# Row sums of a 64 MiB tensor: moving six of eight blocks from two engines to VectorE alone

## The chip, the cores and the metric

The kernel runs on one core of one Trainium2 chip. The metric is the device time of one execution in microseconds (us); a profile shows a span about 1.8 us shorter. Before the change the median was 162.4 us (162.32 to 162.68). All runs, each on one core, were at a granted clock of 1.0. They come from three chips; where a ratio is given, both kernels ran on the same chip in the same rounds.

Engine names in the profiles: DVE is VectorE, ACT is ScalarE, SPq is the sequencer of SyncE, which issues the DMAs. L92 is line 92 of that kernel; lines move by two or more between kernels. A *landing* is the moment when a whole block has arrived; it is read here as the start of DVE's reduction of that block, since DVE waits for each one.

## The reference

```python
x = np.random.randn(32, 512, 1024).astype(np.float32)      # 16384 rows, 67.1 MB
out = (np.sum(x, axis=-1) * 0.5).astype(np.float32)        # one number per row, 64 KB
```

Every input byte is read once and used for one addition, so the first question is how well the loads are kept running.

## The kernel before

The rows are laid over 128 partitions, 128 rows on each, in 8 blocks of 16 rows a partition (8.39 MB a block). A pool of three buffers holds the blocks. A load is one DMA of a whole block (64 KB for each partition); the last block comes in five pieces so that little is left to do after the last byte. In each block DVE reduces half the rows in one instruction, and ACT the other half, one row per instruction (a copy with scale whose accumulator gives the sum).

```python
B = 16                                       # rows of a partition in one block
x_pool = ctx.enter_context(tc.tile_pool(name="x", bufs=3))
# ... (cut: sums, res, part; act_row: one nc.scalar.activation(..., accum_out=res[:, col]) per row)
for b in range(n_blocks - 1):                # blocks 0 to 6
    c0 = b * B
    t = x_pool.tile([P, B, D], fp32, name="xb")
    loads.append(nc.sync.dma_start(out=t, in_=x_rows[:, c0 : c0 + B, :]))
    h = B // 2
    nc.vector.reduce_sum(out=sums[:, c0 : c0 + h], in_=t[:, 0:h, :], axis=mybir.AxisListType.X)
    nc.vector.tensor_single_scalar(out=res[:, c0 : c0 + h], in_=sums[:, c0 : c0 + h],
                                   scalar=mul, op=mybir.AluOpType.mult)
    for r in range(h, B):
        act_row(t, r, c0 + r)
# ... (cut: block 7 in five loads; 7 rows on ACT, the others on DVE; two stores)
```

A buffer may be loaded again when both engines have finished with it. With three buffers, the load of block b+3 is issued when block b is summed, while the loads of blocks b+1 and b+2 are already in the DMA queue.

Of the kernel before, what the change touches and what calls it, by code (L numbers as in the profile page):

```python
# [1 line left out]

# [4 lines left out]


@with_exitstack
def kernel(  # L10
    ctx: ExitStack,
    tc: tile.TileContext,
    x: bass.AP,
    multiplier: float,
    out: bass.AP,
):








    nc = tc.nc
    P = nc.NUM_PARTITIONS
    fp32 = mybir.dt.float32
    ADD = mybir.AluOpType.add

    x_flat = x.flatten_outer_dims()  # L30
    N, D = x_flat.shape
    rows = N // P
    out_flat = out.rearrange("b s -> (b s)")
    mul = float(multiplier)

    B = 16
    n_blocks = rows // B
    assert N == P * rows and rows == n_blocks * B
    own = rows - B
    x_rows = x_flat[0 : P * own, :].rearrange("(p c) d -> p c d", p=P)  # L40
    x_last = x_flat[P * own : N, :].rearrange("(p c) d -> p c d", p=P)
    out_rows = out_flat[0 : P * own].rearrange("(p c) -> p c", p=P)
    out_last = out_flat[P * own : N].rearrange("(p c) -> p c", p=P)

    x_pool = ctx.enter_context(tc.tile_pool(name="x", bufs=3))
    res_pool = ctx.enter_context(tc.tile_pool(name="res", bufs=1))
    sums = res_pool.tile([P, rows], fp32, name="sums")
    res = res_pool.tile([P, rows], fp32, name="res")
    part = res_pool.tile([P, 1], fp32, name="part")

    SYNC = mybir.DependencyInfo(mybir.DependencyClass.Sync, mybir.DependencyReason.DATA)
    ORDER = mybir.DependencyInfo(
        mybir.DependencyClass.NoSync, mybir.DependencyReason.SCHED_ONLY
    )

    def nop_after(engine, waits_for, follows):
        i = engine.nop()
        for w in waits_for:
            tc.add_manual_dep(i.ins, w.ins.name, SYNC, reason="end seen here")
        for f in follows:  # L60
            tc.add_manual_dep(i.ins, f.ins.name, ORDER, reason="in this order")
        return i

    loads = []
    acts = []

    def act_row(t, r, col):
        acts.append(nc.scalar.activation(  # L68
            out=t[:, r, :],
            in_=t[:, r, :],  # L70
            func=mybir.ActivationFunctionType.Copy,
            scale=mul,
            accum_out=res[:, col : col + 1],
        ))

    def dve_span(t, r, lo, hi, dst, start=0.0):
        mid = (lo + hi) // 2
        return nc.vector.tensor_tensor_reduce(  # L78
            out=t[:, r, lo:mid],
            in0=t[:, r, lo:mid],  # L80
            in1=t[:, r, mid:hi],
            scale=mul,
            scalar=start,
            op0=ADD,
            op1=ADD,
            accum_out=dst,
        )

    for b in range(n_blocks - 1):
        c0 = b * B  # L90
        t = x_pool.tile([P, B, D], fp32, name="xb")
        loads.append(nc.sync.dma_start(out=t, in_=x_rows[:, c0 : c0 + B, :]))  # L92
        h = B // 2
        nc.vector.reduce_sum(  # L94
            out=sums[:, c0 : c0 + h], in_=t[:, 0:h, :], axis=mybir.AxisListType.X
        )
        nc.vector.tensor_single_scalar(  # L97
            out=res[:, c0 : c0 + h],
            in_=sums[:, c0 : c0 + h],
            scalar=mul,  # L100
            op=mybir.AluOpType.mult,
        )
        for r in range(h, B):
            act_row(t, r, c0 + r)

    c0 = (n_blocks - 1) * B
    t = x_pool.tile([P, B, D], fp32, name="xb")
    cut = 576
    pieces = [(0, 8), (8, 13), (13, 15)]
    for lo, hi in pieces:  # L110
        loads.append(
            nc.sync.dma_start(  # L112
                out=t[:, lo:hi, :], in_=x_last[:, lo:hi, :]
            )
        )
    for lo, hi in ((0, cut), (cut, D)):
        loads.append(
            nc.sync.dma_start(  # L118
                out=t[:, B - 1, lo:hi], in_=x_last[:, B - 1, lo:hi]
            )  # L120
        )
    early = nc.sync.dma_start(out=out_rows, in_=res[:, 0:own])
    on_act = {4, 5, 6, 7, 11, 12, 14}
    for r in range(B - 1):
        if r in on_act:
            act_row(t, r, c0 + r)
        else:
            dve_span(t, r, 0, D, res[:, c0 + r : c0 + r + 1])
    dve_span(t, B - 1, 0, cut, part)
    final = dve_span(t, B - 1, cut, D, res[:, rows - 1 : rows], start=part)  # L130




    seen = nop_after(nc.sync, loads[-8:] + acts[-1:], [])
    store = nc.sync.dma_start(out=out_last, in_=res[:, own:])
    tc.add_manual_dep(store.ins, seen.ins.name, ORDER, reason="in this order")
    for a in acts[-len(on_act) :]:
        tc.declare_no_dep(store.ins, a.ins.name, reason="waited for by the nop in front")
    nop_after(nc.sync, [early, final], [store])  # L140

    def start_loads_at_entry(nc_):



        entry, *rest = nc_.main_func.blocks
        is_sp = lambda i: i.engine == mybir.EngineType.SP
        is_load = lambda i: type(i).__name__ == "InstDMACopy"
        for block in rest:
            body = list(block.instructions)  # L150
            own = [i for i in body if is_sp(i)]
            if not any(is_load(i) for i in own):
                continue
            lead = []
            for i in own:
                if not is_load(i) or i.sync_info.on_wait:
                    break
                lead.append(i)
            names = {i.name for i in lead}
            block.instructions = [i for i in body if i.name not in names]  # L160
            head = list(entry.instructions)
            at = next(
                k for k, i in enumerate(head) if is_sp(i) and type(i).__name__ == "InstDrain"
            )
            entry.instructions = head[:at] + lead + head[at:]
            return

    nc.at_finalize(start_loads_at_entry)


# [1 line left out]
_INS = ['x', 'multiplier']  # L172
_OUTS = [((32, 512), 'float32')]

_NUMBERS = {'multiplier': 0.5}


# [26 lines left out]
```

## Time and profile before

| | before |
|---|---|
| time, median | 162.4 us |
| DVE busy, ACT busy | 68.1 us, 67.9 us of a 160.6 us span |
| one block: from landing to landing | 19.35 us (one of the six intervals: 19.71) |
| one block: DVE's reduction | 8.69 us |
| reload issued after the landing of its buffer's block | 8.8 us |

The first lines are from the page of the kernel before: busy times; DMA queues; the chain of work that ended last, by engine; and the two costliest groups of instructions, where the number after the bar is busy time and the mean of one in ns, and behind the next bar the idle time in front of them and what ended it.

```profile
DVE 68.1 (42%) x34; ACT 67.9 (42%) x127; POOL 0.2 (0%) x4
...
q1 hardware_dynamic: 2016, 67.18, 97.4%
q14 instruction: 1, 0.01, 0.0%
...
DMA 86%; DVE 11%; SPq 1%; issue 0%; DVEq 0%
...
L68 ACT ACTIVATE xb<-xb 128x1024 f32<-128x1024 f32 x63 | 65.6, 1043 | 88.1 <-DMA xb<-in_x_dram 88.1
L94 DVE TENSOR_REDUCE sums<-xb 128x8 f32<-128x8192 f32 x7 | 60.8, 8686 | 84.9 <-DMA xb<-in_x_dram 84.9
```

Neither engine is busy half of the time, and what each waits for, 85 to 88 us in all, is the next load. The data queue takes 97.4% of the DMA engines' time. So the loads set the time. Note also the second queue: one packet of 0.01 MB on a queue called "instruction".

Next, windows of the kernel before, cut at four landings. A line has the window and its length, then the busy time of DVE, ACT and POOL, the granted clock, the share of the DMA engines and their rate in GB/s.

```profile
41.14:60.49 19.35, 8.86 (x2) 8.43 (x16) 0.00 (x0) 1.00 1.00 434
60.49:79.86 19.37, 8.86 (x3) 8.42 (x16) 0.00 (x0) 1.00 1.00 433
79.86:99.57 19.71, 8.86 (x3) 8.42 (x16) 0.00 (x0) 1.00 0.98 426
99.57:118.92 19.35, 8.86 (x3) 8.43 (x16) 0.00 (x0) 1.00 1.00 434
```

The DMA engines are full (1.00) at 434 GB/s. The Trainium skill, "DMA: Bandwidth & Descriptors", Specifications, gives 435 GB/s as the ceiling of the path into SBUF; this trace agrees with it. One interval is 0.36 us longer than the others.

The timeline of the kernel before around block 1 shows how a buffer comes free (columns: start, length, engine, line, operation; the idle time before in brackets).

```profile
41.14 8.69 DVE L94 TENSOR_REDUCE sums<-xb 128x8 f32<-128x8192 f32 x1 [10.43 <-DMA xb<-in_x_dram]
49.86 0.17 DVE L97 TENSOR_SCALAR res<-sums 128x8 f32<-128x8 f32 x1
49.91 0.33 SPq L92 DMA_DIRECT2D xb<-in_x_dram  x1
60.49 8.69 DVE L94 TENSOR_REDUCE sums<-xb 128x8 f32<-128x8192 f32 x1 [10.46 <-DMA xb<-in_x_dram]
```

Block 1 lands at 41.14, its sum ends 8.7 us later, and the reload of its buffer is issued at 49.91. At that moment 60.49 - 49.91 = 10.6 us of block 2's load are left, and all of block 3's, 19.35 us: 30 us of queued transfers. DVE then idles 10.4 us.

### The profile page before, as it was taken

How to read it: one execution, taken by the hardware profiler on the slowest of the kernel's cores; microseconds unless marked ns; L12 is line 12 of the kernel's file. 1: busy time of each engine (PE TensorE's matmuls, PEld its weight loads, DVE VectorE, ACT ScalarE, POOL GpSimd, SP SyncE). 2: the span in 40 equal slices, each digit the busy share in tenths (PEclk: the TensorE clock that was granted, in tenths of full speed). 3: DMA queues.
4: the chain of work that ended last, by engine and by line, in shares of the span. 5: the costliest groups of instructions: out<-in, count | busy, mean ns of one | idle time of the engine just before them, and what ended most of it. 6: DMA issues, size and time to landing. Idle time of an engine off the chain costs nothing.

```text
span 160.6 us, 236 instructions
## 1 busy us (share of the span) xinstructions
DVE 68.1 (42%) x34; ACT 67.9 (42%) x127; POOL 0.2 (0%) x4
## 2 busy tenths in 40 slices
DVE  0000059600794009920199002990039800597543
ACT  3000059500793009910099001990039700596952
POOL 0000000000000000000000000000000000000000
DMA  7996996996996996996996996996997997999991
GB/s 261 522 522 261 522 522 261 522 522 261 522 522 261 522 522 261 522 522 261 522 524 261 522 490 294 522 490 294 522 473 310 522 441 343 392 473 409 418 374 39
DMA packets 2017, 67.18 MB, mean 418 GB/s; under 512 B 480, under 2 KB 608, under 8 KB 736
## 3 DMA queue, kind: packets, MB, share of 16 engines
q1 hardware_dynamic: 2016, 67.18, 97.4%
q14 instruction: 1, 0.01, 0.0%
HBM read 67.11 MB, written 0.07 MB: 418 GB/s over the span
## 4 chain that ended last, share of the span: by engine, by line
DMA 86%; DVE 11%; SPq 1%; issue 0%; DVEq 0%
DMA xb<-in_x_dram 86%; DVE sums L94 11%; SPq L112 1%; DVE xb L78 0%; SPq L118 0%; SPq L92 0%; DVEq L78 0%; DVEq L199 0%
## 5 line engine op out<-in xcount | busy, mean ns | idle before, releaser
L68 ACT ACTIVATE xb<-xb 128x1024 f32<-128x1024 f32 x63 | 65.6, 1043 | 88.1 <-DMA xb<-in_x_dram 88.1
L94 DVE TENSOR_REDUCE sums<-xb 128x8 f32<-128x8192 f32 x7 | 60.8, 8686 | 84.9 <-DMA xb<-in_x_dram 84.9
L68 ACT ACTIVATION_READ_ACCUMULATOR xb<-xb 128x1 f32 x63 | 11.8, 187 | 0.0
L78 DVE CUSTOM_DVE_ANT_0 xb<-xb 128x512 f32<-128x512 f32 (+1 forms) x9 | 5.6, 663 | 5.0 <-DMA xb<-in_x_dram 5.0
L68 ACT ACT_TABLE_LOAD x1 | 1.3, 1283 | 1.7 <-PEq L185 1.7
L97 DVE TENSOR_SCALAR res<-sums 128x8 f32<-128x8 f32 x7 | 1.2, 172 | 0.2
L78 DVE DVE_READ_ACCUMULATOR2_ANT res<- 128x1 f32 x9 | 0.7, 83 | 0.0
L78 DVE CUSTOM_DVE_ANT_0 xb<-xb,part 128x224 f32<-128x224 f32 x1 | 0.5, 452 | 0.2 <-DMA xb<-in_x_dram 0.2
L185 POOL MEMSET const-bfloat16-1.0<- 128x1 bf16 x1 | 0.1, 101 | 0.0
L185 POOL MEMSET const-uint8-127<- 128x1 uint8 x1 | 0.1, 101 | 0.0
L185 POOL MEMSET const-float32-0.0<- 128x1 f32 x1 | 0.1, 98 | 0.2 <-issue 0.2
L185 POOL MEMSET const-float32-1.0<- 128x1 f32 x1 | 0.1, 98 | 0.0
L78 DVE DVE_READ_ACCUMULATOR2_ANT part<- 128x1 f32 x1 | 0.1, 84 | 0.0
## 6 DMA issues: line engine op xcount, KB each, us to landing
xb<-in_x_dram SPq DMA_DIRECT2D x1, 4096.0 KB, 39.6
xb<-in_x_dram SPq DMA_DIRECT2D x1, 2560.0 KB, 45.4
xb<-in_x_dram SPq DMA_DIRECT2D x1, 1024.0 KB, 47.4
xb<-in_x_dram SPq DMA_DIRECT2D x1, 288.0 KB, 47.6
xb<-in_x_dram SPq DMA_DIRECT2D x1, 224.0 KB, 47.7
xb<-in_x_dram SPq DMA_DIRECT2D x7, 49.6
out_dram<-res SPq DMA_DIRECT2D x1, 56.0 KB, 10.8
out_dram<-res SPq DMA_DIRECT2D x1, 8.0 KB, 1.4
```

Of the source, the lines that this page charges most:

```text
L68: acts.append(nc.scalar.activation(out=t[:, r, :], in_=t[:, r, :], func=mybir.ActivationFunctionType.Copy, scale=mul, accum_out=res[:, col ...
L78: return nc.vector.tensor_tensor_reduce(out=t[:, r, lo:mid], in0=t[:, r, lo:mid], in1=t[:, r, mid:hi], scale=mul, scalar=start, op0=ADD, o ...
L94: nc.vector.reduce_sum(out=sums[:, c0 : c0 + h], in_=t[:, 0:h, :], axis=mybir.AxisListType.X)
L97: nc.vector.tensor_single_scalar(out=res[:, c0 : c0 + h], in_=sums[:, c0 : c0 + h], scalar=mul, op=mybir.AluOpType.mult,)
L112: nc.sync.dma_start(out=t[:, lo:hi, :], in_=x_last[:, lo:hi, :])
L185: nc = _bacc.Bacc("TRN2", target_bir_lowering=False, num_devices=1)
```

## The change

The intent: DVE, which idles more than half of each block, takes all 16 rows of blocks 0 to 5 in one instruction each. ACT is left with 15 rows in blocks 6 and 7, that is 15 ACTIVATEs with 15 accumulator reads: 30 instructions instead of 126. In the last two blocks both engines share the work as before, to keep the end short.

```diff
-        h = B // 2
+        h = B if b < n_blocks - 2 else B // 2
         nc.vector.reduce_sum(
             out=sums[:, c0 : c0 + h], in_=t[:, 0:h, :], axis=mybir.AxisListType.X
         )
```

(Two blank lines are added too. Nothing else differs.)

## The prediction

> **What bounds the kernel now.** The input DMA. The chain of waits is 86% DMA into xb; its DVE pieces stand only where more loads were queued anyway. Landings, read as the starts of the reductions in the timeline: 21.82, 41.14, 60.49, 79.86, 99.57, 118.92, 138.27 us: one 8.39 MB block per 19.35 us, 433 GB/s. The Trainium skill, "DMA: Bandwidth & Descriptors", Specifications, gives a fabric ceiling of 435 GB/s; the trace agrees. DVE and ACT are 42% busy each (busy table) and wait about 10.4 us per block for the next load (groups: 84.9 and 88.1 us idle on DMA).
>
> **What the change does.** In blocks 0 to 5 DVE reduces 128x16384 instead of 128x8192; ACT loses 48 ACTIVATEs (1.04 us a row) and their accumulator reads. Blocks 6 and 7, all loads, both stores and the tail keep their instructions. The 128x8192 reduction took 8.69 us, so double the length costs at most 17.37 us (estimate; 17.2 if some of it is fixed), plus 0.17 us for the scaling: about 17.6 to 17.9 us per block, under the 19.35 us between landings. DVE keeps up, idle 1.5 to 2 us per block. Its busy time rises from 68.1 to about 120 us (75%); ACT's falls from 67.9 to about 17 us.
>
> **What of it is critical.** Nothing on DVE. A buffer comes free, and its reload is issued, about 17.4 us after landing instead of 8.7. At that moment the queue still holds 2 us of the next block and one whole block: about 21 us of transfers (30 before), against 1 us from issue to first byte (the trace's first packets). The queue never runs dry. The last block's pieces are issued near 117 instead of 108.3 us, 21 us ahead of need. The sum of block 5 ends near 136, before block 6 lands at 138. From there on nothing changes: ACT and DVE are both free when block 6 lands.
>
> **One small gain.** One interval between landings is 19.71 us, not 19.35. In the DMA records a single 8 KB packet of the instruction queue starts at 83.90 us, and one data packet just behind it takes 2.78 instead of 2.42 us; every later landing is 0.36 us later. ACT is the engine that works through many instructions there (127 in all). The Trainium skill, "Runtime: NRT & Kernel Launch", Instruction fetch mechanics, says that each engine fetches its next block of instructions by DMA while it runs. With 30 ACT instructions and a table load that fetch should not happen: minus 0.36 us. I give this 70%.
>
> **Prediction.** 162.1 us (162.4 - 0.3 expected), 161.6 to 162.8 at 8 in 10. Faster by over 2%: 0.01; within 2%: 0.98; slower: 0.01.
>
> **What would show each step.** Six DVE reductions of about 17.3 us and one of 8.69; DVE's idle before them 1.5 to 2 us, ended by DMA; landings every 19.35 us from 21.82 on; the DMA row of the slices full as before; no packet on the instruction queue and no 19.71 us interval (last landing near 157.5 instead of 157.85); span about 160.2.
>
> **What would make it wrong.** A reduction that costs more than linearly, over 19 us: then DVE sets the pace. DMA that needs two whole loads queued to hold its rate: then intervals grow once reloads move later. Reading by DVE during the whole transfer slowing the writes: not seen before, where intervals with engine work equal the first block's transfer without any. The fetch belonging to another engine, or moving elsewhere: then 162.4.

## The result

The changed kernel took 162.28 us, median of 6 runs (162.12 to 162.41), against 162.39 us for the kernel before (162.32 to 162.68, 6 runs). The ratio is 0.9991 with a 95% interval from 0.9978 to 1.0004: the same within 2%, and by these runs alone not clearly different from 1. (A ratio is the mean time of one kernel's fast runs over that of the other's of the same rounds, so it is not quite the ratio of the medians quoted.)

The same parts of the page, for the changed kernel:

```profile
DVE 119.3 (74%) x34; ACT 17.3 (11%) x31; POOL 0.2 (0%) x4
...
q1 hardware_dynamic: 2016, 67.18, 97.5%
...
DMA 75%; DVE 22%; SPq 1%; issue 0%; DVEq 0%
```

Its costliest groups, from the list that keeps shapes apart, so that the six long reductions stand alone:

```profile
L96 DVE TENSOR_REDUCE sums<-xb 128x16 f32<-128x16384 f32 x6 | 103.3, 17220 | 31.6 <-DMA xb<-in_x_dram 31.6
L70 ACT ACTIVATE xb<-xb 128x1024 f32<-128x1024 f32 x15 | 15.7, 1045 | 2.1 <-DMA xb<-in_x_dram 2.1
L96 DVE TENSOR_REDUCE sums<-xb 128x8 f32<-128x8192 f32 x1 | 8.7, 8687 | 1.9 <-DMA xb<-in_x_dram 1.9
```

DVE's busy time went up by 51 us, ACT's down by 51 us, and the span by 0.1 us. In front of its reductions DVE still waits, and for the DMA: it never falls behind. The line of the instruction queue is gone.

One trap for a reader: DVE's share of the chain doubled from 11% to 22%, which looks as if DVE had become critical. The chain is followed back from a landing to the issue of that load, and from there to the sum that freed the buffer. That sum really released the issue, but the load then stood in the queue behind others. A link of such a chain costs time only if the queue ran dry before that load could start.

The windows of the changed kernel, between the same landings:

```profile
41.38:60.73 19.35, 17.39 (x2) 0.00 (x0) 0.00 (x0) 1.00 1.00 434
60.73:80.09 19.36, 17.39 (x2) 0.00 (x0) 0.00 (x0) 1.00 1.00 433
80.09:99.44 19.35, 17.39 (x2) 0.00 (x0) 0.00 (x0) 1.00 1.00 434
99.44:118.78 19.34, 17.39 (x2) 0.00 (x0) 0.00 (x0) 1.00 1.00 434
```

Double the DVE work, no ACT work, the same 19.35 us; the long interval is missing. From the first landing to the seventh it is 138.27 - 21.82 = 116.45 us before and 138.13 - 22.05 = 116.08 after: 0.37 us less. The span shows only 0.1 us of it because in this execution the first block landed 0.23 us later. First landings lie between 21.81 and 22.05 us in all profiles but one (tiny600, below), with no pattern by kernel; I take that as scatter between executions.

And the timeline of the changed kernel around block 1:

```profile
41.38 17.22 DVE L96 TENSOR_REDUCE sums<-xb 128x16 f32<-128x16384 f32 x1 [1.90 <-DMA xb<-in_x_dram]
58.63 0.33 SPq L94 DMA_DIRECT2D xb<-in_x_dram  x1
58.64 0.17 DVE L99 TENSOR_SCALAR res<-sums 128x16 f32<-128x16 f32 x1
60.73 17.22 DVE L96 TENSOR_REDUCE sums<-xb 128x16 f32<-128x16384 f32 x1 [1.92 <-DMA xb<-in_x_dram]
```

The reload is issued 17.25 us after the landing, with 2.1 us of block 2's load and all of block 3's ahead of it: 21.4 us of transfers instead of 30. DVE's idle time per block fell from 10.4 to 1.9 us.

One thing moved that was not foreseen. ACT's lines in the timeline, at the start of block 6 and of the last block; first the kernel before:

```profile
138.35 1.06 ACT L68 ACTIVATE xb<-xb 128x1024 f32<-128x1024 f32 x1 [10.93 <-DMA xb<-in_x_dram]
...
148.06 1.06 ACT L68 ACTIVATE xb<-xb 128x1024 f32<-128x1024 f32 x1 [1.29 <-DMA xb<-in_x_dram]
```

The same two places in the changed kernel:

```profile
138.20 1.28 ACT L70 ACT_TABLE_LOAD   x1 [138.20 <-DMA xb<-in_x_dram]
139.50 1.06 ACT L70 ACTIVATE xb<-xb 128x1024 f32<-128x1024 f32 x1
...
147.93 1.06 ACT L70 ACTIVATE xb<-xb 128x1024 f32<-128x1024 f32 x1
```

Before, the table load ran at 1.73 us. After, ACT's first arithmetic instruction is in block 6; it has several semaphores (counters that signal finished work) to wait for, and the program puts the waits for the loads ahead of the table load in front of it. So the 1.28 us now stand behind block 6's landing. They used up ACT's 1.29 us of waiting before the last block, no more.

### The profile page after: what moved, and what is told of

Same layout as the page of the kernel before. It is cut to its first block, busy times and chain, and to the rows that moved or that the text cites. A ratio compares the mean times of both kernels' runs of the same rounds, so it can differ in the third digit from the quotient of the medians.

```text
span 160.5 us, 138 instructions
## 1 busy us (share of the span) xinstructions
DVE 119.3 (74%) x34; ACT 17.3 (11%) x31; POOL 0.2 (0%) x4
## 4 chain that ended last, share of the span: by engine, by line
DMA 75%; DVE 22%; SPq 1%; issue 0%; DVEq 0%
DMA xb<-in_x_dram 75%; DVE sums L96 21%; SPq L114 1%; DVE xb L80 0%; SPq L120 0%; SPq L94 0%; DVE res L99 0%; DVEq L80 0%; DVEq L201 0%
## 5 line engine op out<-in xcount | busy, mean ns | idle before, releaser
L96 DVE TENSOR_REDUCE sums<-xb 128x16 f32<-128x16384 f32 (+1 forms) x7 | 112.0, 16001 | 33.6 <-DMA xb<-in_x_dram 33.6
L70 ACT ACT_TABLE_LOAD x1 | 1.3, 1283 | 138.2 <-DMA xb<-in_x_dram 138.2
L70 ACT ACTIVATE xb<-xb 128x1024 f32<-128x1024 f32 x15 | 15.7, 1045 | 2.1 <-DMA xb<-in_x_dram 2.1
L70 ACT ACTIVATION_READ_ACCUMULATOR xb<-xb 128x1 f32 x15 | 2.8, 187 | 0.0
L99 DVE TENSOR_SCALAR res<-sums 128x16 f32<-128x16 f32 (+1 forms) x7 | 1.2, 174 | 0.2
```

The costliest lines, as they stand in the source:

```text
L70: acts.append(nc.scalar.activation(out=t[:, r, :], in_=t[:, r, :], func=mybir.ActivationFunctionType.Copy, scale=mul, accum_out=res[:, col ...
```

## The experiments

Theory: the input DMA sets the time. Doubling DVE's work and delaying the reloads costs nothing as long as DVE needs less than 19.35 us per block and the queue holds something; the only change on the critical path is the missing packet of ACT's program. Rivals: the two halves of the change affect the loads in opposite ways and cancel; the 0.1 us is noise; the changed kernel is already at an edge.

| run | what it is | time, median (before, same rounds) | ratio, 95% interval |
|---|---|---|---|
| after_again | the changed kernel | 162.16 (162.43) | 0.9985 [0.9973, 0.9998] |
| dve8_no_act | ACT's work removed alone | 162.19 (162.43) | 0.9986 [0.9973, 0.9998] |
| dve16_act8 | DVE's work added alone | 162.40 (162.43) | 1.0001 [0.9987, 1.0015] |
| early_table | changed, table load early | 162.10 (162.43) | 0.9982 [0.9969, 0.9994] |
| tiny600 | changed, 600 tiny ACT instructions | 165.03 (162.47) | 1.0161 [1.0147, 1.0174] |
| dve_plus1 | changed, DVE +1 row per block | 162.25 (162.47) | 0.9988 [0.9975, 1.0002] |
| dve_plus4 | changed, DVE +4 rows per block | 169.69 (162.47) | 1.0446 [1.0431, 1.0460] |
| before_bufs2 | before, two buffers | 162.44 (162.38) | 1.0004 [0.9991, 1.0016] |
| after_bufs2 | changed, two buffers | 170.60 (162.38) | 1.0502 [1.0486, 1.0518] |
| before_bufs1 | before, one buffer | 240.95 (162.38) | 1.4830 [1.4807, 1.4853] |
| after_bufs1 | changed, one buffer | 292.95 (162.38) | 1.8045 [1.8020, 1.8069] |
| dve14_bufs2 | two buffers, 14 rows on DVE | 162.51 (162.45) | 1.0006 [0.9992, 1.0020] |

All gave correct results except dve8_no_act, which leaves rows out on purpose.

### Is there a small gain, and which half of the change gives it?

after_again is the changed kernel, no edit.

> The changed kernel once more, to see whether 0.1 us of gain stands. Theory (the input DMA sets the time; the one change on its path is the missing 8 KB instruction packet, worth 0.28 to 0.36 us; the first landing varies by some 0.2 us from run to run): median 162.0 to 162.35, 0.05 to 0.35 us under the kernel before; no packet of the instruction queue in the span; seven landings 19.35 us apart. Rival (the 0.11 us is noise): medians within 0.05 us of each other.

Measured: 162.16 against 162.43 us, an interval wholly below 1. With the first six runs the gain is 0.11 and 0.27 us by the medians of the two sets. It stands, but only just, and its size is no better known than "0.1 to 0.3 us".

The halves of the change, each alone. dve8_no_act is the kernel before without ACT in blocks 0 to 5:

```diff
-        for r in range(h, B):
+        for r in range(h if b == n_blocks - 2 else B, B):
             act_row(t, r, c0 + r)
+        if b < n_blocks - 2:
+            nc.vector.memset(res[:, c0 + h : c0 + B], 0.0)
```

> The removal alone: in blocks 0 to 5 DVE sums 8 rows as before, ACT does nothing, and the other 8 rows are set to zero (wrong result on purpose). Theory: the same as the changed kernel within 0.15 us, no instruction packet, landings 19.35 us apart, although DVE does half the work. Rival (the two halves of the change cancel: less ACT traffic speeds the loads, longer DVE reading slows them): clearly faster than both kernels, landings under 19.2 us apart.

dve16_act8 is the changed kernel in which ACT still goes over rows 8 to 15 of each block, into a scratch tile:

```diff
         for r in range(h, B):
             act_row(t, r, c0 + r)
+        if h == B:
+            for r in range(B // 2, B):
+                nc.scalar.activation(out=junk, in_=t[:, r, :], func=Copy,
+                                     scale=mul, accum_out=junk_sum[:, c0 + r : c0 + r + 1])
```

> The addition alone: DVE sums all 16 rows in blocks 0 to 5 as in the changed kernel, and ACT still goes over its 8 rows, into a scratch tile (right result). Theory: the same as the kernel before within 0.15 us (about 162.4), the instruction packet back once, near the same place in ACT's program, with one data packet of about 2.8 us just behind it and one interval between landings 0.2 to 0.4 us longer; the others 19.35. Rival (the halves cancel): slower than the kernel before by 0.5 us or more, all intervals longer than 19.35.

Measured: the time goes with ACT's instructions and not at all with DVE's work. Without ACT's rows it is 162.19 (DVE 8 rows) and 162.16 (16 rows); with them 162.43 (8) and 162.40 (16). Landings in dve8_no_act are 19.33 to 19.36 us apart, not under 19.2, so the loads don't run faster when DVE reads less: the halves do not cancel, and that rival falls. Its queue list has no instruction packet, and where the kernel before had its long interval it has this one:

```profile
79.97 8.69 DVE L94 TENSOR_REDUCE sums<-xb 128x8 f32<-128x8192 f32 x1 [10.45 <-DMA xb<-in_x_dram]
88.69 0.17 DVE L97 TENSOR_SCALAR res<-sums 128x8 f32<-128x8 f32 x1
99.33 8.69 DVE L94 TENSOR_REDUCE sums<-xb 128x8 f32<-128x8192 f32 x1 [10.46 <-DMA xb<-in_x_dram]
```

In dve16_act8 the packet is back. From its queue list:

```profile
q14 instruction: 1, 0.01, 0.0%
```

And DVE's timeline around it:

```profile
80.01 17.22 DVE L98 TENSOR_REDUCE sums<-xb 128x16 f32<-128x16384 f32 x1 [1.92 <-DMA xb<-in_x_dram]
97.27 0.17 DVE L101 TENSOR_SCALAR res<-sums 128x16 f32<-128x16 f32 x1
99.47 17.22 DVE L98 TENSOR_REDUCE sums<-xb 128x16 f32<-128x16384 f32 x1 [2.03 <-DMA xb<-in_x_dram]
```

This interval is 19.46 us, 0.11 longer than the others, where 0.2 to 0.4 had been expected (0.36 before). The DMA records of the two traces say why. A DMA engine moves packets of 64 KB back to back, 2.418 us each; the numbers are the start, length and end of a packet in us:

```
kernel before                                          dve16_act8
data packet, ends                83.908                data packet, ends                86.288
instruction packet  83.901 0.309 84.210                instruction packet  86.284 0.309 86.593
next data packet    84.207 2.782 86.989                next data packet    86.590 2.721 89.311
latest of the other engines      86.716                latest of the other engines      89.239
```

The packet costs its DMA engine twice: 0.30 us for itself, and 0.30 to 0.36 us more on the data packet behind it, together 0.61 to 0.66 us. But a block has landed only when all 16 engines have delivered (the Trainium skill, "DMA: Bandwidth & Descriptors", Why a DMA increments its semaphore by 16 and not by 1; in these traces DVE starts 0.34 to 0.49 us after the end of the last engine's packet), and this engine was ahead of the slowest one, by 0.39 us before and by 0.54 us in dve16_act8. It ended 0.27 and 0.07 us after the others, and that is the part that can reach the landing. (The landings themselves moved by 0.36 and 0.11, a little more in both; what makes up the remaining 0.04 to 0.09 us was not found.) So the cost of the packet depends on the chance order of the engines.

### Does the packet belong to ACT's program, and does its cost add up?

tiny600 adds 600 ACT instructions of one column to the changed kernel, ahead of the loop. They touch no loaded data.

```diff
+    for k in range(600):
+        nc.scalar.activation(out=tout[:, k : k + 1], in_=tin, func=Copy, scale=mul)
```

> The changed kernel with 600 ACT instructions of one column each ahead of the loop: they read nothing that the loads bring and end before block 6. Theory (the packets of the instruction queue fetch ACT's program, and one costs up to 0.36 us where it lands on a DMA engine that then comes last): 4 to 6 packets of 8 KB instead of none, each with one data packet of about 2.7 to 2.8 us behind it; 163.4 to 164.4 us if they all fall to the same DMA engine, 162.4 to 162.9 if they are spread over the engines, since only the slowest of the 16 sets the landing. Rival (the packet belongs to another engine or to the profile): no packets, 162.2 us.

Measured: 165.03 us, above the highest figure expected, with five packets. The queue list of tiny600:

```profile
q1 hardware_dynamic: 2016, 67.18, 95.6%
q14 instruction: 5, 0.04, 0.1%
```

Its DVE timeline, the first four reductions:

```profile
23.11 17.22 DVE L104 TENSOR_REDUCE sums<-xb 128x16 f32<-128x16384 f32 x1 [21.25 <-DMA xb<-in_x_dram]
...
43.00 17.22 DVE L104 TENSOR_REDUCE sums<-xb 128x16 f32<-128x16384 f32 x1 [2.47 <-DMA xb<-in_x_dram]
...
63.70 17.22 DVE L104 TENSOR_REDUCE sums<-xb 128x16 f32<-128x16384 f32 x1 [3.27 <-DMA xb<-in_x_dram]
...
83.06 17.22 DVE L104 TENSOR_REDUCE sums<-xb 128x16 f32<-128x16384 f32 x1 [1.93 <-DMA xb<-in_x_dram]
```

Until ACT's tiny instructions end at 59 us, the landings come late: 23.11 instead of about 21.9, then intervals of 19.89 and 20.70; from there on 19.36 again. The five packets start at 11.58, 21.79, 34.58, 47.36 and 57.71 us, two, one and two before the three late landings. The data packet right behind the first took 2.66 us, those behind the other four 2.80 us. The seventh landing comes at 141.13 instead of 137.93 us in the profile of after_again, 3.2 us later; five times 0.30 us for the packets, and 0.24 + 4 x 0.38 us for the data packets behind them, make 3.3 us. So almost every packet counted in full. That is what happens when all fall to one and the same DMA engine, and the trace shows it: the records name no engine, but when each packet is followed to the one that starts where it ends, all five lie in one chain. That engine ends its part of the seventh block at 140.65 us, the other fifteen between 136.98 and 137.55 us. The expectation was short because it reckoned 0.36 us per packet, the longer data packet alone, and left out the 0.30 us of the packet itself.

The packet is ACT's instruction fetch: it comes back with ACT's instructions (dve16_act8), goes with them (dve8_no_act) and multiplies with them. The Trainium skill, "Runtime: NRT & Kernel Launch", Instruction fetch mechanics, says that an engine fetches its next page of instructions by DMA while it executes the current one; these runs agree. The 0.05 to 0.35 us expected of the changed kernel hold.

### Does the late table load take anything back?

early_table adds one such tiny instruction to the changed kernel, so that the table load comes ahead of it, at 1.72 us.

> The changed kernel with one tiny ACT instruction ahead of the loop, so that the table load runs early again instead of at 138.2 us in front of block 6. Theory: ACT starts block 6 near 138.2 instead of 139.5 us and waits 1.2 us for the last block again; the time stays that of the changed kernel within 0.1 us, because the late load only used up that wait. Rival (the late table load took back part of the gain): 0.15 us or more faster than the changed kernel.

Measured: 162.10 against 162.16 us, inside the 0.1 us expected. ACT starts block 6 at 138.02 us and has 1.30 us of waiting before the last block again. The late load cost nothing that these runs can show; it used up a wait.

### How much room has DVE left?

dve_plus1 and dve_plus4 add to the changed kernel, in blocks 0 to 5, a second reduction whose result is not used.

```diff
+        if h == B:
+            nc.vector.reduce_sum(out=junk_sum[:, 0:4], in_=t[:, 0:4, :],   # dve_plus1: 0:1
+                                 axis=mybir.AxisListType.X)
```

> The changed kernel with one more row reduced by DVE in each of blocks 0 to 5 (a second reduction of about 1.2 us, result unused). DVE then needs about 18.7 us per block. Theory (DVE has 1.9 us per block to spare, and its longer hold on the buffers costs nothing while a load stays queued): the time of the changed kernel, 162.0 to 162.4. Rival (the changed kernel is already at the edge through the later reloads): 163 us or more.

> The changed kernel with four more rows reduced by DVE in each of blocks 0 to 5, about 4.4 us: DVE needs about 21.9 us per block, 2.5 us over the interval between landings. Theory: DVE now falls behind by 2.5 us per block, ends block 5 near 153.5 us, and everything after is DVE alone (8.9 us for block 6, about 6.3 us for its part of the last block): 171.5 to 174 us, while the landings stay about 19.35 us apart, because each reload is still issued 6 us or more before the queue runs dry. Rival (later reloads hurt the DMA): landings move apart, 175 us or more.

Measured: one row more, 162.25 us, nothing. Four rows more, 169.69 us: slower, as the theory has it, but less than the 171.5 expected at least. DVE's timeline of dve_plus4:

```profile
21.85 17.22 DVE L97 TENSOR_REDUCE sums<-xb 128x16 f32<-128x16384 f32 x1 [21.85 <-DMA xb<-in_x_dram]
38.99 4.41 DVE L101 TENSOR_REDUCE junk_sum<-xb 128x4 f32<-128x4096 f32 x1
43.31 0.16 DVE L104 TENSOR_SCALAR res<-sums 128x16 f32<-128x16 f32 x1
43.39 17.21 DVE L97 TENSOR_REDUCE sums<-xb 128x16 f32<-128x16384 f32 x1
```

DVE no longer waits for a load after the first (no bracket), and a block takes 43.39 - 21.85 = 21.54 us, 2.2 over the DMA's pace. I had put it at 21.9; instructions that don't wait overlap by about 0.08 us, and there is no delay between landing and start. Block 5's sum ends at 151.0 instead of 153.5 us, which accounts for the miss. The DMA records of this run show the blocks still ending 19.33 to 19.37 us apart: DVE falls behind and the loads do not. This is the cliff that the change moved towards: past 19.35 us per block, the excess of each of the six blocks adds up.

### What do the later reloads cost?

Two buffers instead of three, for both kernels:

```diff
-    x_pool = ctx.enter_context(tc.tile_pool(name="x", bufs=3))
+    x_pool = ctx.enter_context(tc.tile_pool(name="x", bufs=2))
```

> The kernel before with two x buffers instead of three. A reload is issued 8.7 us after a landing, when about 10.6 us of the next load are left to run and nothing is queued behind it. Theory (the queue only has to have something left for about 1 us): the time of the kernel before, 162.2 to 162.7. Rival (the loads hold their rate only with a whole load queued behind the running one): slower by 2 us or more.

> The changed kernel with two x buffers. A reload is issued 17.25 us after a landing, when the running load has 2.1 us to the landing that DVE sees, but the first DMA engines run out about 1.0 us before that, and the first byte takes about 1.0 us from the issue. Theory: just at the edge, 0 to 0.3 us lost per reload, 162.1 to 164.0 us. With two buffers the change has eaten nearly all of the slack of the buffers (10.6 us before). Rival (a whole load must be queued): slower by 2 us or more.

Measured: the kernel before does not mind, 162.44 us. So the loads need no whole block queued behind the running one. The changed kernel with two buffers loses 8.2 us and misses my expectation (162.1 to 164.0) by far. Its timeline:

```profile
41.29 17.22 DVE L96 TENSOR_REDUCE sums<-xb 128x16 f32<-128x16384 f32 x1 [1.92 <-DMA xb<-in_x_dram]
...
63.09 17.22 DVE L96 TENSOR_REDUCE sums<-xb 128x16 f32<-128x16384 f32 x1 [4.38 <-DMA xb<-in_x_dram]
...
82.76 17.22 DVE L96 TENSOR_REDUCE sums<-xb 128x16 f32<-128x16384 f32 x1 [2.24 <-DMA xb<-in_x_dram]
```

Every second interval is long: 21.80, 19.67, 21.94, 19.33 and 22.31 us after the first, 8.3 us in excess of five times 19.35, which is the whole loss. The DMA records show what I had mis-sized. The reload of 39.19 us came 1.1 us before the first DMA engine ran dry (40.32) and 1.7 before the last (40.86). The 16 engines began it between 40.68 and 42.37 us, 1.5 to 3.2 us after the issue; in the worst case (issue at 121.94, 0.4 us after the first engine had run dry) between 1.0 and 3.9 us. I had taken the 1.0 us of the first engine at the start of the program for all 16. Besides, their first packets took 2.95 us on average instead of 2.42.

To tell this start-up from any other effect of holding a buffer longer, dve14_bufs2 keeps two buffers but gives DVE 14 rows and ACT 2:

```diff
-        h = B if b < n_blocks - 2 else B // 2
+        h = B - 2 if b < n_blocks - 2 else B // 2
```

> Two x buffers again, but DVE takes 14 rows of blocks 0 to 5 and ACT 2, so that a reload is issued 15.1 us after a landing instead of 17.25. In the two-buffer run with 16 rows the reload came 1.1 us before the first DMA engine ran dry, and its 16 engines started only 1.5 to 3.9 us after the issue. Theory (what was lost there was this start-up of a queue that had run dry, nothing else about the longer reduction): here the first engine runs dry 3.3 us and the last 3.9 us after the issue, so nearly all engines find the next packet waiting: 162.1 to 163.0 us, landings 19.35 to 19.45 us apart, all six. Rival (with one buffer fewer any long hold costs, in proportion): about 8 us times 15.1/17.25, 169 us; or about half of the 8 us, if the loss falls gradually with the time of the issue.

Measured: 162.51 us, the time of the kernel before. The timeline shows the reload issued at 36.97, 15.2 us after the landing, 3.2 us before the first engine runs dry at 40.19, and the next landing in time:

```profile
36.97 0.33 SPq L94 DMA_DIRECT2D xb<-in_x_dram  x1
...
41.16 15.09 DVE L96 TENSOR_REDUCE sums<-xb 128x14 f32<-128x14336 f32 x1 [4.05 <-DMA xb<-in_x_dram]
```

All intervals are 19.32 to 19.42 us, where 19.35 to 19.45 had been expected. A load issued 3.2 us before the first engine runs dry loses next to nothing; one issued 1.1 us before loses 2.4 us. Two in after_bufs2 were issued 2.0 us before (58.54 and 100.01 us): one lost 0.3 us, the other nothing. But these two followed a gap that had spread the engines, so that the last one ran dry only 4.2 and 4.3 us after the issue. So the edge lies somewhere between 1.1 and 3.2 us, and the loss is not in proportion to the time that a buffer is held. (This run has an instruction packet too, at 152.28 us, after 49 ACT instructions; its last load packet ends 0.27 us later than in after_again.)

### What would the change cost with nothing to hide it?

One buffer (bufs=1), for both kernels: a load starts only after the sum of the block before.

> The kernel before with one x buffer: loads and sums take turns, so nothing is hidden. Theory: 21.8 us from issue to landing plus 8.73 us of summing per block, seven times, then a last load of about 22 us and the tail: about 240 us (236 to 244).

> The changed kernel with one x buffer. Theory: each of blocks 0 to 5 costs 8.5 us more than with one buffer before the change, and block 6 about 1 us more because the table load now stands in front of ACT's rows: about 52 us over the kernel before with one buffer, about 292 us (287 to 297). That is what the change costs where nothing hides it.

Measured: 240.95 and 292.95 us, as expected. The change costs 52.0 us where load and sum take turns; six times the longer reduction, 6 x (17.22 - 8.69), is 51.2. With three buffers the same 51 us cost nothing. A lone load takes 21.7 to 22.1 us from issue to landing instead of the 19.35 us of a running stream, the start-up again.

## Why the prediction was right

It was right in the time (162.1 us predicted, range 161.6 to 162.8; 162.28 and 162.16 measured) and in the class. Point by point:

- **The DMA bounds the kernel.** Shown: landings stay 19.35 us apart with DVE at 8 or 16 rows and ACT with or without work (dve8_no_act, dve16_act8, after), but for the intervals with an instruction packet.
- **DVE needs 17.6 to 17.9 us per block and keeps up.** The reduction took 17.22 us, the low end of the estimate (17.2 to 17.37), idle 1.9 us. dve_plus1 and dve_plus4 show that the room is real and where it ends.
- **The later reload is harmless because 21 us are queued.** Right for three buffers. The figure beside it, "1 us from issue to first byte", was too small a measure of what a reload needs: with two buffers the 16 engines started 1.0 to 3.9 us after the issue. It didn't matter here only because 21 us is much more than either.
- **The instruction packet vanishes: minus 0.36 us.** It vanished, and it was ACT's. The term was mis-sized: what was read as the packet's cost, 2.78 instead of 2.42 us on one data packet, is about half of what its engine loses (0.66 us), and of that only the part by which the engine becomes the slowest counts. 0.36 us is what one execution showed on its landings. The packet came again in other executions: it lengthened an interval by 0.32 us in before_bufs2, by 0.11 us in dve16_act8, and by nothing that shows in before_bufs1, where it ran at 115.45 us while no load was under way. The medians moved by 0.11 and 0.27 us. The prediction's 0.3 expected was right in size partly by luck.
- **"From there on nothing changes."** Not quite: the table load moved behind the landing of block 6. It filled a wait of the same length, and early_table shows no cost.

Still open: why the data packet behind a fetch takes 0.24 to 0.38 us longer; what the last hundredths between packet end and landing are; and the gain to better than 0.1 us. No version clearly beat the changed kernel: early_table at 162.10 us is within its scatter.

## What to carry to other kernels

When a stream of loads bounds a kernel, as here, compute moved between engines cost nothing until one engine's time per block exceeded the interval between landings (dve_plus4), or until a reload was issued so late that the queue ran dry (after_bufs2); measure both distances (here 1.9 and 21 us) before and after such a change, since it may spend nearly all of one at no visible cost. A DMA chain in a profile that passes through a compute engine proves an order, not a cost: ask how full the queue was. And when differences of 0.2% matter, look for packets on the instruction queue: ACT with 31 instructions fetched nothing during the run, with 127 it fetched once, and with 631 five times.

## What the Trainium skill lacked or had wrong

- "Runtime: NRT & Kernel Launch", Instruction fetch mechanics: it has refills of 16 KiB, "mostly hidden". Here they were packets of 8 KB, one about every 123 ACT instructions (11.5 us apart at 0.0935 us each in tiny600). Hidden from ACT (the 600 tiny instructions start at most 0.11 us apart), but not from a kernel bound by loads: each cost the DMA engine that it came to 0.54 to 0.68 us, and five moved the landings by 3.2 us.
- "DMA: Bandwidth & Descriptors", Specifications: first-byte latency of about 0.6 us. That agrees here if it is counted from the end of the issuing instruction (0.33 to 0.38 us long); from its start the first packet came after 1.0 us. The page doesn't say that the engines start apart: on an idle queue the sixteenth started 1.3 to 2.1 us after the start of the issue, and after a queue ran dry in mid-stream the engines started 1.0 to 3.9 us after it, with first packets of 2.95 to 3.14 instead of 2.42 us. The page has no figure for how early a load must be issued to keep a stream unbroken: 3.2 us was enough here, 1.1 us was not.
- "SBUF — State Buffer", Summary: rules for kernel authors, advises about 358 GB/s for HBM to SBUF. One core alone streamed at 434 GB/s here; "HBM Reference", Specifications (TRN2), has the distinction between a lone core and a pair.
- "ScalarE: Activation LUTs", What ACT_TABLE_LOAD costs, does not say that the load may stand behind the semaphore waits of the first activation. It did here, so 1.28 us that ran at 1.7 us before ran at 138.2 us after the change.
